# A two-layer decoder trunk: gate and up products with the activations stationary, the FFN's pre-gain in the weights, bias products over 128 rows, and eight weight splits on GpSimd

## The chip, the cores and the metric

The kernel runs on one core of a Trainium2 chip. The metric is device microseconds of one execution. Lower is better. TensorE runs at one of two clock levels, 1.2 or 2.4 GHz; the profile gives the granted clock as a share of 2.4 GHz.

## The reference

The input is 256 rows of 1024 numbers. Two layers follow one another; each is FFN, mixer, FFN, and every sub-layer has an RMS norm before and after it. Cut to what matters here:

```python
def rms_norm(x, g):
    y = x * rsqrt(mean(x * x, axis=-1) + 1e-6)
    return y * g

def swiglu_ffn(h, w_gate_up, w_down):            # 1024 -> 2 x 2816 -> 1024
    gate, up = split(h @ w_gate_up, 2)
    return (silu(gate) * up) @ w_down

for layer in range(2):
    x = x + 0.5 * rms_norm(swiglu_ffn(rms_norm(x, fpre[layer, 0]), ...), fpost[layer, 0])
    h = rms_norm(x, mpre[layer])
    y = conformer_conv(h) if layer == 0 else attention(h, shared_kv(x))
    x = x + rms_norm(y, mpost[layer])
    x = x + 0.5 * rms_norm(swiglu_ffn(rms_norm(x, fpre[layer, 1]), ...), fpost[layer, 1])
```

The convolution layer is `(h @ w_in + b_in)` with a gate, a depthwise convolution of 31 taps, a layer norm, and `silu(u) @ w_out + b_out`. All is float32.

## The kernel before

**Products.** A float32 product is made of three products of a faster format (fp32r): each operand is split into a high part and a low part, and `mm3` (lines 185 to 189) adds high x high, high x low and low x high into one PSUM tile. The high part is a copy by ScalarE, the low part a subtraction by VectorE.

**Weights.** All weights lie in one tensor `wpk` of 320 pieces of 128 x 1024 numbers (512 KB), in the order in which `plan` (line 56) lists them. SyncE's queue loads a piece into one of 4 `raw` buffers (line 154); `split_piece` makes `whi` (ScalarE, line 172) and `wlo` (VectorE, line 174), two halves of 512 columns each, into one of 9 pairs of buffers. For the keys `k`, `q`, `v` of the attention the split also multiplies by a norm's gain (lines 167 and 168). `use` (line 177) loads and splits up to 10 pieces ahead of the one asked for. A `raw` buffer is free again when its split is done, a split buffer when TensorE has read it for the last time.

**The FFN** (`ffn`, line 296) has 22 blocks of 128 hidden columns. The normed rows stand transposed in `xT` (high and low, 1024 x 256). `gate_up` (line 324) makes one block for both halves of the rows at once: `unit` (line 275) keeps a 128 x 128 block of weights in the array and moves 256 columns of `xT` past it, 48 matmuls for a block. The result `pgu` stands already transposed, as the down product wants it: a silu, a product, a split, and it is `act`. The first block of the first FFN and the first three of the others are made by `gate_up_rows` (line 302) instead, one half of the rows (`tt`) at a time: there the rows are stationary, 256 columns of weights move, and two transposes a block (`pta`, line 318) turn the result. That lets the FFN begin when the first half of the rows is ready; `turn` (line 238) transposes the rows (`ptr`, line 244) into `xT`.

**The down product** (`down`, line 339) has the activations stationary and moves 512 columns of weights; it follows its block by two blocks or more. Of the second half of the rows the last 7 blocks (`DEFER`) are put off to the end, where they cover the norms of the first half.

**Norms.** `chain` (line 379) makes the sub-layer's end for a half of the rows: `post_norm` (line 207) adds the normed result into `xs`, and `pre_norm` (line 223) scales `xs` by the reciprocal root (made by GpSimd, line 198) and, before an FFN, by the gain: `xg`, line 233, which `turn` transposes. A gain row is loaded by a DMA that repeats it over 128 partitions.

**The convolution layer** (`conv`, line 430) adds its biases by a matmul over 33 partitions (`bhl`, lines 450 and 523): the high part of the bias in one row, the low part 32 rows below, against ones. Its 16 input pieces (`cin`) are followed by 8 output pieces (`cout`). `filter_` makes the convolution by a Fourier product (`pU`, `prod`, `ys`, `y`), `layer_norm` normalizes `y` into `z`, and its reciprocal root `re` is made by GpSimd (line 503).

The instructions of an engine run in the order of its queue. A scheduler sets that order from the program's order and from priorities (`high_priority`, `issue_after`).

Of the kernel before, what the change touches and what calls it, by code (L numbers as in the profile page):

```python
# [47 lines left out]
GAINS_AT = 10  # L48
POOL_SPLITS = ()
VTURN = 1  # L50
FTURN = 7
FLEAD = (1, 3, 3, 3)
# [3 lines left out]
def plan():  # L56

    order = []
    for f in (0, 1, 2, 3):
        for i in range(NF):  # L60
            order += [("gu", f, i, 0), ("gu", f, i, 1)]
            if i % 2 == 1 and i >= 3:
                order += [("dn", f, i - 3), ("dn", f, i - 2)]
# [5 lines left out]
        if f == 2:  # L69
# [9 lines left out]
GAINS = ["fpre0", "fpost0", "mpre0", "mpost0", "fpre1", "fpost1",  # L79
         "fpre2", "fpost2", "mpost1", "fpre3", "fpost3"]  # L80
# [17 lines left out]
def trunk(ctx, tc, x, wpk, gains, pvec, dft, wdw, bvec, out):  # L98
# [5 lines left out]
    t2 = ctx.enter_context(tc.tile_pool(name="t2", bufs=12))  # L104
    gpool = ctx.enter_context(tc.tile_pool(name="gpool", bufs=3))
# [29 lines left out]

    load_x(0)
    pv = const.tile([P, NPV], F32, name="pv")
    load_gain("fpre0")
# [9 lines left out]
    def load_piece():  # L148

        i = state["next"]  # L150
        state["next"] += 1
        key = order[i]
        raw = wraw.tile([P, HW], F32, name="raw", tag="raw")
        nc.sync.dma_start(raw, wpk[i])
        return lambda: split_piece(key, raw, nc.gpsimd if i in POOL_SPLITS else nc.vector)

    def split_piece(key, raw, eng):
# [3 lines left out]
        if key[0] in ("k", "q", "v"):  # L161
            gname = "gq" if key[0] == "q" else "gkv"
            parts = [(key[1], 0, HW)] if key[0] == "v" else [
                (4 * key[2] + j, 256 * j, 256) for j in range(4)]
            for k, o, n in parts:
                g = pcol(gname, k)
# [34 lines left out]
    def sumsq(src):  # L201
        junk = t2.tile([P, 512], F32, name="junk", tag="junk", bufs=1)
# [18 lines left out]
    normed = {}  # L221

    def pre_norm(tt, pre):
# [51 lines left out]
    def unit(p, w):  # L275

        for s in range(2):
            for k in range(KD):
                wh, wl = w[k // 4]
                c = ((k % 4) * 2 + s) * P  # L280
                mm3(p[:, s, :], wh[:, c:c + P], wl[:, c:c + P], xT[0][:, k, :], xT[1][:, k, :],
                    k == 0, k == KD - 1)

    def rows_unit(p, w, tt, final):


        for k in range(KD):
            if final and tt == 0 and k == FTURN:
                turn(1)
# [526 lines left out]
```

## Time and profile before

| | |
|---|---|
| runs | 996.59, 998.08, 999.80 us; median 998.08 |
| the profiled execution | 997.41 us |
| its span from the first to the last instruction | 995.6 us |
| TensorE matmul busy | 976.5 us (98% of the span) |
| VectorE busy | 605.5 us (61%) |
| ScalarE busy | 517.4 us (52%) |
| GpSimd busy | 19.1 us (2%) |
| HBM | 175.14 MB read, 177 GB/s over the span |
| granted TensorE clock | 0.996 in the mean, 0.5 in a stretch near the start |

The busy time of TensorE counts a matmul from its issue to its modelled end, and matmuls overlap. What a matmul costs is the distance from its start to the start of the next.

### The profile page before, as it was taken

The numbers are of one execution on the slowest core, as the hardware profiler recorded it, in microseconds if no ns is written. First come the engines' busy times: TensorE is split into PE (matmuls) and PEld (weight loads), VectorE is DVE, ScalarE is ACT, GpSimd is POOL, SyncE is SP. The second block draws the span as 40 slices with busy tenths as digits, with TensorE's granted clock in tenths as the row PEclk, the third lists the DMA queues.
The fourth block names the chain that finished last, engine by engine and source line by source line (L and its number), as shares of the span: only waits on it lengthen the run. The fifth ranks groups of instructions, "written<-read, shape, count | busy, mean of one in ns | idle before, by whom it ended". The sixth has DMA issues, their size and how long they took to land.

```text
span 995.6 us, 16742 instructions
## 1 busy us (share of the span) xinstructions
PE 976.5 (98%) x6470; PEld 884.3 (89%) x6470; DVE 605.5 (61%) x1136; ACT 517.4 (52%) x1083; POOL 19.1 (2%) x40
## 2 busy tenths in 40 slices
PE   7999999999989999999999999999999999999997
PEld 6998999976658999999899999998899899999996
DVE  5865454487568654545585454547887785454542
ACT  5755454473246554544564454546785565454541
POOL 0000000010001000000000000000000000000000
PEclk8999999999999999999999999999999999999999
DMA  6867565565226766665476566655654456666531
GB/s 234 293 216 245 156 173 187 162 198 169 92 78 211 214 190 189 181 198 165 141 240 206 184 190 191 173 162 185 202 160 122 142 172 210 190 180 199 172 106 43
DMA packets 49232, 177.27 MB, mean 178 GB/s; under 512 B 5593, under 2 KB 5593, under 8 KB 49152
## 3 DMA queue, kind: packets, MB, share of 16 engines
q1 hardware_dynamic: 49152, 176.21, 57.0%
q8 instruction: 50, 0.82, 0.3%
q14 instruction: 30, 0.25, 0.1%
HBM read 175.14 MB, written 1.05 MB: 177 GB/s over the span
## 4 chain that ended last, share of the span: by engine, by line
PE 89%; DVE 4%; DMA 2%; issue 2%; ACT 1%; POOL 1%; DVEq 0%; SPq 0%; POOLq 0%; ACTq 0%
PE pgu L187 15%; PE pgu L189 15%; PE pgu L188 15%; PE acc L271 9%; PE acc L272 9%; PE acc L273 9%; PE pgr L189 1%; PE pgr L187 1%; PE pgr L188 1%; PE pkq L189 1%; PE pkq L188 1%; PE pkq L187 1%; PE pag L187 1%; DVE wlo L174 1%; DMA raw<-in_wpk_dram 1%
## 5 line engine op out<-in xcount | busy, mean ns | idle before, releaser
L174 DVE TENSOR_TENSOR wlo<-raw,whi 128x512 fp32r<-128x512 f32 x592 | 389.3, 687 | 297.7 <-ACT whi L172 286.7
L172 ACT CAST whi<-raw 128x512 fp32r<-128x512 f32 x592 | 344.5, 618 | 334.1 <-PE pgu L188 124.6
L188 PE MATMUL pgu<-xTl,whi 128*128 128x256 f32 x1248 | 353.3, 283 | 0.2 <-DVE xTl L255 0.2
L189 PE MATMUL pgu<-xTh,wlo 128*128 128x256 f32 x1248 | 353.4, 283 | 0.0
L187 PE MATMUL pgu<-xTh,whi 128*128 128x256 f32 x1248 | 353.2, 283 | 0.0
L187 PEld LDWEIGHTS pgu<-xTh,whi 128*128 128x128 f32 x1248 | 239.5, 192 | 2.2 <-issue 0.8
L188 PEld LDWEIGHTS pgu<-xTl,whi 128*128 128x128 f32 x1248 | 239.4, 192 | 1.8 <-DVE xTl L255 0.4
L189 PEld LDWEIGHTS pgu<-xTh,wlo 128*128 128x128 f32 x1248 | 239.4, 192 | 0.0
L271 PE MATMUL acc<-whi,act 128*128 128x512 f32 x384 | 150.4, 392 | 0.0
L272 PE MATMUL acc<-whi,act 128*128 128x512 f32 x384 | 150.1, 391 | 0.0
L273 PE MATMUL acc<-wlo,act 128*128 128x512 f32 x384 | 149.6, 390 | 0.0
L273 PEld LDWEIGHTS acc<-wlo,act 128*128 128x128 f32 x384 | 72.1, 188 | 15.2
L271 PEld LDWEIGHTS acc<-whi,act 128*128 128x128 f32 x384 | 72.3, 188 | 13.7
L272 PEld LDWEIGHTS acc<-whi,act 128*128 128x128 f32 x384 | 72.3, 188 | 13.1
L188 PE MATMUL pgr<-wlo,xTh 128*128 128x256 f32 x160 | 46.7, 293 | 0.2 <-DVE wlo L174 0.2
L187 PE MATMUL pgr<-whi,xTh 128*128 128x256 f32 x160 | 46.5, 292 | 0.2 <-ACT whi L172 0.2
L189 PE MATMUL pgr<-whi,xTl 128*128 128x256 f32 x160 | 45.8, 291 | 0.1
L333 ACT CAST act<-af 128x256 fp32r<-128x256 f32 x78 | 31.7, 407 | 23.9 <-DVE af L331 23.8
L167 ACT ACTIVATE whi<-raw,pv 128x256 fp32r<-128x256 f32 (+1 forms) x72 | 36.5, 573 | 7.5 <-PE pgu L188 2.5
L168 DVE SCALAR_TENSOR_TENSOR wlo<-raw,pv,whi 128x256 fp32r<-128x256 f32 (+1 forms) x72 | 37.2, 568 | 5.0 <-ACT whi L167 5.0
L188 PE MATMUL pkq<-xTl,whi 128*128 128x256 f32 x128 | 36.5, 285 | 0.0
L187 PE MATMUL pkq<-xTh,whi 128*128 128x256 f32 x128 | 36.5, 285 | 0.0
(125 smaller groups left out, 949.0 us busy)
## 6 DMA issues: line engine op xcount, KB each, us to landing
raw<-in_wpk_dram SPq DMA_DIRECT2D x320, 512.0 KB, 4.3
gain<-in_gains_dram SPq DMA_DIRECT2D x11, 512.0 KB, 5.8
xs<-in_x_dram SPq DMA_DIRECT2D x4, 256.0 KB, 2.7
out_dram<-xs SPq DMA_DIRECT2D x4, 256.0 KB, 2.0
dm<-in_dft_dram SPq DMA_DIRECT2D x1, 368.0 KB
taps<-in_wdw_dram SPq DMA_DIRECT2D x1, 124.0 KB
braw<-in_bvec_dram SPq DMA_DIRECT2D x6, 4.0 KB
ys<-in_bvec_dram SPq DMA_DIRECT2D x2, 2.0 KB
```

The costliest lines, as they stand in the source:

```text
L167: nc.scalar.activation(hi[:, o:o + n], raw[:, o:o + n], AF.Copy, scale=g)
L168: nc.vector.scalar_tensor_tensor(lo[:, o:o + n], raw[:, o:o + n], g, hb[:, o:o + n], op0=ALU.mult, op1=ALU.subtract)
L172: nc.scalar.copy(hi[:, o:o + 512], raw[:, o:o + 512])
L174: eng.tensor_sub(lo[:, o:o + 512], raw[:, o:o + 512], hb[:, o:o + 512])
L187: nc.tensor.matmul(out_ap, wh, xh, start=start, stop=False)
L188: nc.tensor.matmul(out_ap, wh, xl, start=False, stop=False)
L189: nc.tensor.matmul(out_ap, wl, xh, start=False, stop=stop)
L271: nc.tensor.matmul(o, xh, wh[:, cols], start=first, stop=False)
L272: nc.tensor.matmul(o, xl, wh[:, cols], start=False, stop=False)
L273: nc.tensor.matmul(o, xh, wl[:, cols], start=False, stop=last)
L333: nc.scalar.copy(hl[:, 0, :], a)
```

## The change

**FFN.** All blocks are now made by `gate_up` in pairs (256 gate and 256 up columns), one half of the rows at a time, with the rows stationary and 512 columns of weights moving. A pair takes 4 pieces, each with two k-blocks of 512 columns, and both halves of the rows read them. `turn_act` transposes the pair's product (4 transposes of 128 x 128, now for every pair), and one copy and one subtraction of 512 columns make `ahi` and `alo`. The FFN's pre-norm no longer makes `xg`: `turn` transposes `xs` as it is; the gain is multiplied into the gate and up weights in the split (a column `gc` of a small table), and the reciprocal root `rstds` into the silu and the product after it. The first pair (first FFN) or two pairs (the others) are made for the first half of the rows, then `turn(1)`, then for the second half. At the FFN's end one deferred down block (`COVERED`) is moved ahead of the last pair's down blocks, since these now wait for `turn_act`.

**Bias product.** The ones and the bias rows stand in 128 partitions, filled with zeros, and the matmul takes all 128.

**Splits on GpSimd.** The low parts of the 8 `cout` pieces (16 subtractions of 128 x 512) are made by GpSimd. The memsets for the bias rows go to GpSimd too.

**Buffers and loads.** `t2` has 14 buffers for 12, the gains 2 for 3, `junk` 2 for 1. Four gain rows of 512 KB are no longer loaded.

```diff
-GAINS_AT = 10
-POOL_SPLITS = ()
+GAINS_AT = 5
+POOL_SPLITS = ("cout",)
-FTURN = 7
-FLEAD = (1, 3, 3, 3)
+FLEAD = (1, 2, 2, 2)
+COVERED = 1
...
-        for i in range(NF):
-            order += [("gu", f, i, 0), ("gu", f, i, 1)]
-            if i % 2 == 1 and i >= 3:
-                order += [("dn", f, i - 3), ("dn", f, i - 2)]
+        for i in range(NF // 2):
+            order += [("gu", f, i, q) for q in range(KD // 2)]
+            if i >= 1:
+                order += [("dn", f, 2 * i - 2), ("dn", f, 2 * i - 1)]
...
+    gc = const.tile([P, NGC], F32, name="gc")
+    nc.sync.dma_start(gc, gcol)
     load_x(0)
     pv = const.tile([P, NPV], F32, name="pv")
-    load_gain("fpre0")
...
-        return lambda: split_piece(key, raw, nc.gpsimd if i in POOL_SPLITS else nc.vector)
+        return lambda: split_piece(key, raw, nc.gpsimd if key[0] in POOL_SPLITS else nc.vector)
...
+        if key[0] in ("gu", "k", "q", "v"):
+            if key[0] == "gu":
+                parts = [(gc[:, key[1] * KD + k:key[1] * KD + k + 1], 512 * (k % 2), 512)
+                         for k in (2 * key[3], 2 * key[3] + 1)]
...
+            for g, o, n in parts:
                 nc.scalar.activation(hi[:, o:o + n], raw[:, o:o + n], AF.Copy, scale=g)
                 nc.vector.scalar_tensor_tensor(lo[:, o:o + n], raw[:, o:o + n], g, hb[:, o:o + n],
                                                op0=ALU.mult, op1=ALU.subtract)
...
+        if pre == "ffn":
+            normed[tt] = xs[:, tt, :].rearrange("p (h n) -> p h n", h=2)
         s = [sumsq(xs[:, tt, h * 512:(h + 1) * 512]) for h in range(2)]
-        r, _ = rstd_of(s[0], s[1], 1.0 / D, RMS_EPS)
+        r, last = rstd_of(s[0], s[1], 1.0 / D, RMS_EPS)
+        if pre == "ffn":
+            rstds[tt] = r
+            return last
...
+        def gate_up(i, tt):
+
+            if i not in raws:
+                raws[i] = ([use(("gu", f, i, q)) for q in range(KD // 2)],
+                           t2.tile([P, NT, 2 * P], F32, name="ar", tag="t2"))
+            w, a = raws[i]
+            p = ps.tile([P, 2, 2 * P], F32, name="pgu", tag="mm")
+            rows_unit(p.rearrange("p a b -> p (a b)"), w, tt)
             with tc.high_priority(offset=400):
+                s = t2.tile([P, 2 * P], F32, name="sg", tag="sg", bufs=2)
+                nc.scalar.activation(s, p[:, 0, :], AF.Silu, scale=rstds[tt])
+                nc.vector.scalar_tensor_tensor(a[:, tt, :], p[:, 1, :], rstds[tt], s, op0=ALU.mult, op1=ALU.mult)
+
+        def turn_act(i):
+
+            a = raws.pop(i)[1]
+            pt = ps.tile([P, 2, T], F32, name="pta", tag="tr")
+            for tt in range(NT):
+                for j in range(2):
+                    nc.tensor.transpose(pt[:, j, tt * P:(tt + 1) * P], a[:, tt, j * P:(j + 1) * P], ident)
             with tc.high_priority(offset=400):
+                hi, lo = (t2.tile([P, 2, T], F32R, name=n, tag="t2") for n in ("ahi", "alo"))
+                nc.scalar.copy(hi, pt)
+                nc.vector.tensor_sub(lo, pt, hi.bitcast(F32))
...
+        for i in range(FLEAD[f]):
+            gate_up(i, 0)
+        turn(1)
+        for i in range(FLEAD[f]):
+            gate_up(i, 1)
+            if i:
+                turn_act(i - 1)
+        for i in range(FLEAD[f], NP):
...
+            gate_up(i, 0)
+            turn_act(i - 1)
+            gate_up(i, 1)
+            if i == FLEAD[f]:
+                for j in range(i - 1):
+                    down_pair(j, range(NT))
+            down_pair(i - 1, range(NT))
+        turn_act(NP - 1)
+        late = list(range(NF - DEFER, NF - TAIL))
+        for j in late[:COVERED]:
+            down(j, 1)
+        down_pair(NP - 1, (0,))
         after(0, acc[0])
-        for j in range(NF - DEFER, NF - TAIL):
+        for j in late[COVERED:]:
...
-            nc.tensor.matmul(flat, onesr[at, :], bhl[0][at, (q % 2) * 512:(q % 2 + 1) * 512],
+            nc.tensor.matmul(flat, onesr[:, q // 2, :], bhl[0][:, (q % 2) * 512:(q % 2 + 1) * 512],
...
-                nc.tensor.matmul(acc[tt][h], onesr[:33, :], bhl[1][:, h * 512:(h + 1) * 512],
+                nc.tensor.matmul(acc[tt][h], onesr[:, 0, :], bhl[1][:, h * 512:(h + 1) * 512],
...
-    with tc.issue_after(pre_norm(0, "fpre0").ins):
-        last = turn(0, between=first[:1])
+    pre_norm(0, "ffn")
+    last = turn(0, between=first[:1])
```

**What moves on the engines.** Three places, as the two programs have them.

TensorE in the middle of the second FFN. Before, the gate and up matmuls of a block (`pgu`, 256 columns) go straight over into the down matmuls (`acc`):

```order
L187 MATMUL pgu<-xTh,whi 128x256
L188 MATMUL pgu<-xTl,whi 128x256
L189 MATMUL pgu<-xTh,wlo 128x256
L271 MATMUL acc<-whi,act 128x512
L272 MATMUL acc<-whi,act 128x512
```

Now the four transposes of the pair before (`pta`) stand between the first and the second half of the rows:

```order
L193 MATMUL pgu<-whi,xTl 128x512
L319 MATMUL pta<-ident,ar 128x128 x4
L191 MATMUL pgu<-whi,xTh 128x512
L192 MATMUL pgu<-wlo,xTh 128x512
L193 MATMUL pgu<-whi,xTl 128x512
```

The matmuls have 512 columns for 256 and are half as many, and a pair has 4 transposes that no block there had before.

GpSimd's queue from the first FFN to the attention, as a difference (`rr` and `re` are the reciprocal roots of the norms, `braw` and `ones` the constants of the bias product, `wlo` the low parts):

```order
-L198 TENSOR_TENSOR rr<-rb,nhalf 128x1 x2
-L409 MEMSET ones 97x128
-L198 TENSOR_TENSOR rr<-rb,nhalf 128x1 x4
-L503 TENSOR_TENSOR re<-ve,nhalf 128x1 x2
-L558 IOTA dist 128x256 x2
```

This stood there before. Now the same stretch has the following, which the difference shows as added:

```order
+L422 MEMSET braw 128x1024 x2
+L412 MEMSET ones 128x256
+L416 MEMSET ones 1x128 x4
+L202 TENSOR_TENSOR rr<-rb,nhalf 128x1 x4
+L178 TENSOR_TENSOR wlo<-raw,whi 128x512 x12
+L509 TENSOR_TENSOR re<-ve,nhalf 128x1
+L178 TENSOR_TENSOR wlo<-raw,whi 128x512 x4
+L509 TENSOR_TENSOR re<-ve,nhalf 128x1
```

The first `re` of the layer norm now stands behind twelve of the sixteen subtractions, the second behind all.

VectorE at the layer norm of the convolution layer, where TensorE waits for it (`z` is the normed `y`, `u` the gated input, `prod` and `ys` the convolution's products). Before:

```order
L506 TENSOR_SCALAR z<-y,mv,re 128x512 x2
L174 TENSOR_TENSOR wlo<-raw,whi 128x512 x2
L460 TENSOR_TENSOR u<-pag,sg 128x256
L174 TENSOR_TENSOR wlo<-raw,whi 128x512 x2
L481 TENSOR_TENSOR prod<-pU,spec_1143 80x512
```

Now:

```order
L507 TENSOR_SCALAR ve<-mv 128x1
L512 TENSOR_SCALAR z<-y,mv,re 128x512 x2
L466 TENSOR_TENSOR u<-pag,sg 128x256
L172 SCALAR_TENSOR_TENSOR wlo<-raw,gc,whi 128x512 x2
L487 TENSOR_TENSOR prod<-pU,spec_892 80x512
```

The subtractions ahead of `u` are gone; two of the next FFN's first piece stand ahead of `prod`.

## Rows read from the trace of the kernel before

**Rows 1.** The page: busy time of each engine with its share of the span and its instructions; and the chain that ended last, as shares of the span.

```profile
PE 976.5 (98%) x6470; PEld 884.3 (89%) x6470; DVE 605.5 (61%) x1136; ACT 517.4 (52%) x1083; POOL 19.1 (2%) x40
...
PE 89%; DVE 4%; DMA 2%; issue 2%; ACT 1%; POOL 1%; DVEq 0%; SPq 0%; POOLq 0%; ACTq 0%
```

**Rows 2.** The timeline of TensorE in the second FFN, from one down stretch over 96 gate and up matmuls to the next: start in us, duration in us, engine, line, operation, out<-in, columns.

```profile
403.32 0.40 PE L271 MATMUL acc<-whi,act 128*128 128x512 f32 x1
...
404.71 0.39 PE L271 MATMUL acc<-whi,act 128*128 128x512 f32 x1
...
408.79 0.28 PE L187 MATMUL pgu<-xTh,whi 128*128 128x256 f32 x1
...
420.30 0.40 PE L271 MATMUL acc<-whi,act 128*128 128x512 f32 x1
```

**Rows 3.** Groups of instructions: line, engine, operation, names, shape, count | busy us, mean ns of one | idle us before them. The groups L187 and L189 have the same counts as L188.

```profile
L188 PE MATMUL pgu<-xTl,whi 128*128 128x256 f32 x1248 | 353.3, 283 | 0.2 <-DVE xTl L255 0.2
...
L188 PE MATMUL pgr<-wlo,xTh 128*128 128x256 f32 x160 | 46.7, 293 | 0.2 <-DVE wlo L174 0.2
...
L318 PE MATMUL pta<-ident,ar 128*128 128x128 f32 x20 | 6.1, 303 | 1.8 <-DVE ar L314 1.8
```

**Rows 4.** The timeline of TensorE at the end of the convolution layer, where eight transposes stand in a stream of 512-column matmuls.

```profile
305.69 0.39 PE L273 MATMUL acc<-wlo,xTh 128*128 128x512 f32 x1
305.92 1.03 PE L244 MATMUL ptr<-ident,xg 128*128 128x128 f32 x8
...
307.03 0.40 PE L272 MATMUL acc<-whi,xTl 128*128 128x512 f32 x1
```

**Rows 5.** The timeline of TensorE around one bias matmul of the convolution layer, and the group of all eight.

```profile
230.94 0.39 PE L189 MATMUL pag<-whi,xTl 128*128 128x512 f32 x1
231.26 0.50 PE L450 MATMUL pag<-bhl,onesr 33*128 33x512 f32 x1
231.69 0.50 PE L187 MATMUL pag<-whi,xTh 128*128 128x512 f32 x1
232.02 0.39 PE L188 MATMUL pag<-wlo,xTh 128*128 128x512 f32 x1
```
```profile
L450 PE MATMUL pag<-bhl,onesr 33*128 33x512 f32 x8 | 4.0, 495 | 0.0
```

**Rows 6.** The start: the timeline of all engines (a bracket gives the idle time before and what ended it), and a row of TensorE's timeline from the second block on.

```profile
1.65 0.42 SPq L125 DMA_DIRECT2D gain<-in_gains_dram  x1
...
8.87 1.41 DVE L233 SCALAR_TENSOR_TENSOR xg<-xs,rr,gain 128x512 f32<-128x512 f32 x2 [2.63 <-DMA gain<-in_gains_dram]
9.67 1.66 PE L244 MATMUL ptr<-ident,xg 128*128 128x128 f32 x8 [2.30 <-DVE xg L233]
...
12.37 0.63 ACT L204 ACTIVATE junk<-xs 128x512 f32<-128x512 f32 x1
```
```profile
29.82 0.28 PE L187 MATMUL pgu<-xTh,whi 128*128 128x256 f32 x1
```

**Rows 7.** The start in stretches of 2 us: stretch and length, busy us (count) of TensorE, its weight loads, VectorE, ScalarE and GpSimd, then the granted clock, the share of the DMA engines and GB/s.

```profile
6.00:8.00 2.00, 1.37 (x4) 0.68 (x2) 0.16 (x1) 0.04 (x1) 0.55 (x1) 1.00 0.93 354
...
12.00:14.00 2.00, 1.78 (x9) 1.67 (x9) 1.90 (x5) 2.00 (x5) 0.00 (x0) 0.50 0.84 319
```

**Rows 8.** The chain that ended last at the end of the first FFN: start in us, us, what.

```profile
198.62 0.24 PE acc L273
...
205.69 0.76 DVE xg L233
206.50 0.65 PE ptr L244 x4
```

**Rows 9.** All waits of TensorE for `xg` (us in total, times, longest), and one of them in its timeline, at the start of the second FFN.

```profile
PE ptr L244 <- DVE xg L233: 5.3, 6, 2.3
```
```profile
318.65 1.29 PE L244 MATMUL ptr<-ident,xg 128*128 128x128 f32 x8 [0.69 <-DVE xg L233]
```

**Rows 10.** The layer norm of the convolution layer: the timeline of VectorE, and of ScalarE (the high parts of the second and of the sixth `cout` piece).

```profile
274.21 1.53 DVE L506 TENSOR_SCALAR z<-y,mv,re 128x512 f32<-128x512 f32 x2 [0.66 <-POOL re L503]
275.66 1.28 DVE L174 TENSOR_TENSOR wlo<-raw,whi 128x512 fp32r<-128x512 f32 x2
276.86 0.42 DVE L460 TENSOR_TENSOR u<-pag,sg 128x256 f32<-128x256 f32 x1
...
278.45 2.48 DVE L481 TENSOR_TENSOR prod<-pU,spec 80x512 f32<-80x512 f32 x4
```
```profile
254.31 1.14 ACT L172 CAST whi<-raw 128x512 fp32r<-128x512 f32 x2 [1.63 <-PE pag L189]
...
268.22 1.14 ACT L172 CAST whi<-raw 128x512 fp32r<-128x512 f32 x2 [3.35 <-PE pag L189]
```

**Rows 11.** Durations: groups of VectorE, ScalarE and GpSimd with shapes kept apart, and the DMA of a piece (count, KB each, median us to landing).

```profile
L174 DVE TENSOR_TENSOR wlo<-raw,whi 128x512 fp32r<-128x512 f32 x592 | 389.3, 687 | 297.7 <-ACT whi L172 286.7
...
L168 DVE SCALAR_TENSOR_TENSOR wlo<-raw,pv,whi 128x1024 fp32r<-128x1024 f32 x8 | 10.2, 1280 | 3.1 <-ACT whi L167 3.1
...
L219 DVE SCALAR_TENSOR_TENSOR xs<-pn,rr,xs 128x512 f32<-128x512 f32 x24 | 17.1, 754 | 1.8 <-POOL rr L198 0.6
...
L560 POOL TENSOR_SCALAR_AFFINE_SELECT dist<-dist 128x256 f32<-128x256 f32 x2 | 0.8, 400 | 0.0
```
```profile
raw<-in_wpk_dram SPq DMA_DIRECT2D x320, 512.0 KB, 4.3
```

More of the change, by code (lines that the diff above doesn't have):

```diff
@@ L76, in plan @@
     return order
[L79 to L80 removed]
+GAINS = ["fpost0", "mpre0", "mpost0", "fpost1", "fpost2", "mpost1", "fpost3"]
+NGC = 4 * KD
 PV = {}
@@ L97, in trunk @@
 @with_exitstack
-def trunk(ctx, tc, x, wpk, gains, pvec, dft, wdw, bvec, out):
+def trunk(ctx, tc, x, wpk, gains, gcol, pvec, dft, wdw, bvec, out):
     nc = tc.nc
@@ L273, in rows_product, with rows_unit @@
             nc.tensor.matmul(o, xh, wl[:, cols], start=False, stop=last)
[L275 to L284, printed above, removed]
+    def rows_unit(p, w, tt):
         for k in range(KD):
-            if final and tt == 0 and k == FTURN:
-                turn(1)
-            wh, wl = w[k // 4]
-            c = slice((k % 4) * 2 * P, (k % 4 + 1) * 2 * P)
+            wh, wl = w[k // 2]
+            c = slice((k % 2) * 512, (k % 2 + 1) * 512)
             xh, xl = (xT[j][:, k, tt * P:(tt + 1) * P] for j in range(2))
@@ L324, in gate_up @@
-        def gate_up(i):
-            p = ps.tile([P, 2, T], F32, name="pgu", tag="mm")
-            unit(p, [use(("gu", f, i, hh)) for hh in range(2)])
-            with tc.high_priority(offset=400):
-                s = t2.tile([P, T], F32, name="sg", tag="sg", bufs=2)
-                nc.scalar.activation(s, p[:, 0, :], AF.Silu)
-                a = t2.tile([P, T], F32, name="af", tag="af", bufs=2)
-                nc.vector.tensor_mul(a, s, p[:, 1, :])
-                hl = t2.tile([P, 2, T], F32R, name="act", tag="t2")
-                nc.scalar.copy(hl[:, 0, :], a)
-                nc.vector.tensor_sub(hl[:, 1, :], a, hl[:, 0, :].bitcast(F32))
-            act[i] = hl
+        raws = {}
@@ L342, in down, with down_pair @@
             wh, wl = wd[i]
-            hl = act[i]
-            rows_product(acc, tt, hl[:, 0, tt * P:(tt + 1) * P], hl[:, 1, tt * P:(tt + 1) * P],
-                         wh, wl, i == 0, i == NF - 1, halves)
-        done = 0
+            hi, lo = act[i]
+            cols = slice(tt * P, (tt + 1) * P)
+            rows_product(acc, tt, hi[:, cols], lo[:, cols], wh, wl, i == 0, i == NF - 1, halves)
+        def down_pair(i, tts):
+            for j in (2 * i, 2 * i + 1):
+                for tt in tts:
+                    if tt == 0 or j < NF - DEFER:
+                        down(j, tt)
+        NP = NF // 2
         if 0 in normed:
             turn(0)
-        for tt in range(NT):
-            for i in range(FLEAD[f]):
-                gate_up_rows(i, tt)
-        for i in range(NF):
+        for i in range(FLEAD[f]):
[6 more added lines that the diff above has]
+        for i in range(FLEAD[f], NP):
             if i == GAINS_AT:
```

89 lines of the change are left out of this document (32 added, 57 removed).

## The prediction

> **What bounds the kernel now.** I read the page first. TensorE is busy for 98% of the span, and the chain that ended last runs on it for 89%; VectorE and ScalarE are busy for 61% and 52%, GpSimd for 2% [rows 1]. So TensorE's stream is priced, and every other engine only at the places where TensorE waits. Since busy times overlap (a matmul of 256 columns is given 283 ns, one of 512 columns some 390), I next read the distance from start to start in the middle of an FFN. From 408.79 to 420.30 lie 96 matmuls of 256 columns: 11.51 / 96 = 0.1199 us each. The 18 matmuls of 512 columns from 404.71 to 408.79 take 4.08 us, 0.2267 each, and the 24 from 403.32 take 5.47, 0.2279 each [rows 2]. A column thus costs 0.468 ns at 256 and 0.443 to 0.445 at 512. The third look was at the few stretches in which TensorE doesn't stream: the start, the ends of the FFNs and the layer norm of the convolution layer. The change touches all of them.
>
> **Gate and up.** Removed are 3 x 1248 matmuls `pgu` and 3 x 160 `pgr` [rows 3], 4224 of 256 columns: 4224 x 0.1199 = 506.5 us. Added are 2112 of 512 columns at 0.2275 (between the two values above): 480.5 us. That is **-26.0** (-25.2 to -27.7 by the two values).
>
> **Transposes.** An FFN has 11 pairs with 4 transposes each, 176 in all, against 20 `pta` now [rows 3]: 156 more. Their own row is no price, since the first ones waited. Eight transposes do stand in a running stream of 512-column matmuls: from 305.69 to 307.03 are 1.34 us with two matmuls and eight transposes [rows 4], so 1.34 - 2 x 0.2267 = 0.887, or 0.111 each. 156 x 0.111 = **+17.3**. Four in a row may cost more by one than eight do, as their beginning and end weigh more: a bound is +0.3 per group, which is about half of the 0.65 us that a group of four took alone at an FFN's end [rows 8]. That bound is a rival below. Copies and subtractions of 512 columns replace two of 256 each on ScalarE and VectorE; both have room, and in a pair's middle the down product that needs them comes 24 matmuls (5.4 us) later.
>
> **Bias product.** The matmul over 33 partitions and the one before and the one after it take 232.02 - 230.94 = 1.08 us from start to start; three matmuls of the stream take 0.68 [rows 5]. The row over 33 partitions thus costs 0.40 more than a plain one. If 128 partitions make it plain, eight of them give 3.2 and the four output biases, of which no row stands alone, some 0.3: **-3.5**. The bounds are 0 (the extra belongs to something else, for instance to its place at a product's start) and -4.8 (12 x 0.40). Padding and memsets lie on GpSimd before that layer, where it has nothing to do. The Trainium skill ("TensorE: Matmul & The Clock Gate", section "Why this matters for your kernels") says that a single matmul over 32 partitions takes the same time as one over 128. By this the padding would give nothing and the sum would be 3.5 us worse. The row disagrees.
>
> **The start.** TensorE's first transposes waited 2.30 us for `xg`, and this waited 2.63 for the gain's DMA, issued at 1.65 [rows 6]. Now `xs` is transposed as it lands; the 512 KB of the gain are not loaded, which at the 354 GB/s of that stretch [rows 7] brings every weight piece 512 / 354 = 1.5 us forward. The table of gains is small and goes first. On the other side the clock was at its upper level from 6 to 8 and at its lower level (0.50, 1.2 GHz) from 12 to 14 [rows 7], though TensorE worked in both: work that comes earlier falls into the same slow time in part. A pair also asks for four pieces and for a split with a scale, and ScalarE was full there (2.00 of 2.00 us [rows 7]). Two blocks, 96 matmuls, were done at 29.82 [rows 6]; I expect the first pair, the same work, at about 26.3. **-3.5**: the 2.30 of the wait and most of the 1.5. Bounds: 0 (ScalarE and the slow clock keep all) and -6 (the wait, the 1.41 of `xg` and the 1.5, and a shorter slow stretch).
>
> **Ends and beginnings of FFNs.** At an end the last pair's transposes now stand before its down product. One deferred down block, 6 x 0.2267 = 1.36 us, covers the copy (0.57, half of 1.14 [rows 10]) and the subtraction (0.69 [rows 11]); with three hand-overs at 0.05 to 0.1 (`xg` ended at 206.45, its reader began at 206.50 [rows 8]) and the transposes' own end the cover is short by some 0.3: four times, +1.2. The covering block is taken from those that hide the first half's norm. At the end of the first FFN this norm runs from 198.86 to 206.45 and the transposes follow it at once [rows 8], so it had no slack. The new order leaves two matmuls fewer between the end of the sum and these transposes: 2 x 0.2267 = 0.45, at the convolution and at the attention, the two places where `xg` stays: +0.9. At the three FFN beginnings the scaled rows are no longer on the path: the wait for `xg` there was 0.69 in the row [rows 9], 2.1 for three; I take half, as the other waits in that total are shorter: -1.0. Sum **+1.1**, bounds -3 (all waits for `xg` but the start's, 5.3 - 2.3 [rows 9]) and +6 (1 us more at each of six places).
>
> **Splits.** The subtractions of gate and up become operations with a scalar: 0.64 for 512 columns by the row of 1024 (1.28), 0.75 by another with the same operands, against 0.69 [rows 11]; 352 of them move VectorE by -17 to +24 us of work, which stays beside the stream: 0. The eight `cout` pieces take 16 x 0.69 = 11 us off VectorE and put 16 subtractions on GpSimd. No row shows one there. Nearest are GpSimd's 256 columns at 0.40, 0.80 for 512, and VectorE's 0.69 [rows 11]; I take 0.8. What they could delay is `re`, queued behind twelve of them, for which VectorE (`z`) and behind it TensorE wait. The second piece's high part was ready at 255.45, the sixth's at 269.36, and `re` was due at 273.55, where VectorE began to wait [rows 10]. Ten subtractions in 18.1 us: from 1.8 us each on `re` comes late, and 0.8 is far below. The Trainium skill ("GPSIMD Engine Reference", section 3.1, "Elementwise") gives 4497 ns for 2048 elements of such an operation; a quarter is 1.12 us, an estimate by that page, also below. VectorE, on its side, loses two or four subtractions (1.28 a pair) ahead of `u` and `prod` [rows 10], and gets two of the next FFN in their place. I count **0**, between -1 and +3.
>
> **The sum.** -26.0 + 17.3 - 3.5 - 3.5 + 1.1 = -14.6. The profiled execution took 997.41, 995.6 of it the span, so 982.8; the median of the runs is 0.67 higher: **983.5**.
>
> **The rivals.** (a) All uncertain terms end well: bias -4.8, start -6, ends 0, matmuls at 0.2267: 998.1 - 27.7 + 17.3 - 4.8 - 6 = **977**. For it: the wait for `xg` in the start is large. Against: the slow clock. (b) Start and ends give nothing or cost: start 0, ends +5: 983.5 + 3.5 + 3.9 = **991**. For it: four new hand-overs, each at a place where the cover was measured to be just enough. (c) GpSimd is late, or holds VectorE up: each of 16 subtractions blocks a VectorE operation, of which only those in the layer norm's chain reach TensorE: +3, **987**. The Trainium skill ("SBUF — State Buffer", section "SBUF: two separate sides") describes a port that VectorE and GpSimd share, held by one of them for a whole instruction. No row of before has both at work on such operands, so it is open. (d) The bias matmul stays dear: **987**. (e) No change: a group of four transposes costs 0.3 us more than half of what eight cost. 44 x 0.3 = 13, and -14.6 shrinks to -1.4: **997**. For it: the product stands in PSUM as a whole only after a hand-over, and `pta` must wait for VectorE's product of the half before; against: in the order it stands 24 matmuls behind that, and the eight at 305.92 show no such price. (f) Slower: the weights starve. Both halves of the rows read a pair's four pieces, so 4 of 9 split buffers are held through the first half (24 x 0.2275 = 5.5 us) and none comes free; then they come free one every 1.37 us. A `raw` buffer waits for its split, this for a buffer, and the next load, 4.3 us to landing [rows 11], for `raw`. I count some 3 us of slack between a landing and its use. If each of the some 41 pairs in the steady state waited, from 14.6 / 41 = 0.36 us a pair the gain would be gone, and at 1 us the time is 983.5 + 41 = **1025**. Against it: six pieces a pair are 3.1 MB in 16.8 us, 187 GB/s, where the start moved 354, and the pieces asked for are ten ahead.
>
> **How the numbers follow.** Chances: forecast 0.57; (a) 0.08; (b) 0.10; (c) 0.08; (d) 0.05; (e) 0.08; (f) 0.04. The range of 8 in 10 takes in the forecast with its bounds and (a) to (d): 975 to 993. What this kernel's measurement can tell from no change is 0.3%, 3 us: faster means below 995.1. Faster are the forecast and (a) to (d), 0.88; within 0.3% is (e), 0.08; slower is (f), 0.04.
>
> **What would show each step.** In the profile after: 512-column `pgu` 0.2267 to 0.2279 apart; a group of `pta` 0.44 longer than two matmuls without it (0.75 would be (e)); the bias matmul with its neighbours 0.68, not 1.08; the first pair done near 26.3; idle times of TensorE of about 0.3 behind `pta` at the four FFN ends and 0.6 before `ptr` at the convolution; `z` waiting no longer for `re` than 0.66. Idle times of `pgu` after `whi` or `wlo`, in every pair, would be (f); `pta` waiting for `ar` inside the FFN would make the transposes dearer than 0.111. The forecast is wrong if the distance of the matmuls depends on which operand is stationary more than on the columns.

## The result, and the profile after

The changed kernel takes 981.9 us (median of 4 runs, 980.67 to 983.77), the kernel before 998.51 beside it: a ratio of 0.9837, 95% interval 0.9814 to 0.9860. The profiled execution took 980.67 us with a span of 978.9.

The page of the changed kernel, busy times and chain, as in [rows 1]:

```profile
PE 960.8 (98%) x4514; PEld 787.8 (80%) x4514; DVE 612.5 (63%) x1048; ACT 550.8 (56%) x1029; POOL 43.0 (4%) x62
...
PE 92%; DVE 3%; ACT 2%; DMA 1%; issue 1%; POOL 0%; DVEq 0%; POOLq 0%; ACTq 0%
```

TensorE is still the bound, with 16 us less of it. Where the time went is read by stretches, cut at the starts of the first and last gate and up matmuls in TensorE's timeline (us of the profiled executions):

| stretch | before | after | difference |
|---|---|---|---|
| start to the end of the first pair (two blocks before) | 29.82 | 21.96 | -7.86 |
| rest of gate and up, first FFN | 163.96 | 162.54 | -1.42 |
| end of the first FFN and convolution layer | 115.75 | 118.42 | **+2.67** |
| gate and up, second FFN | 174.49 | 170.47 | -4.02 |
| end of the second FFN | 16.82 | 16.66 | -0.16 |
| gate and up, third FFN | 173.61 | 170.49 | -3.12 |
| end of the third FFN and attention | 125.47 | 125.48 | +0.01 |
| gate and up, fourth FFN | 174.08 | 170.48 | -3.60 |
| end of the fourth FFN | 21.61 | 22.37 | +0.76 |
| sum | 995.61 | 978.87 | -16.74 |

The middle of an FFN, TensorE's timeline, which answers to [rows 2, 4]:

```profile
399.63 0.39 PE L193 MATMUL pgu<-whi,xTl 128*128 128x512 f32 x1
...
404.39 0.39 PE L193 MATMUL pgu<-whi,xTl 128*128 128x512 f32 x1
404.62 0.60 PE L319 MATMUL pta<-ident,ar 128*128 128x128 f32 x4
404.97 0.48 PE L191 MATMUL pgu<-whi,xTh 128*128 128x512 f32 x1
405.29 0.39 PE L192 MATMUL pgu<-wlo,xTh 128*128 128x512 f32 x1
...
410.53 0.39 PE L282 MATMUL acc<-whi,ahi 128*128 128x512 f32 x1
```

From 399.63 to 404.62 are 22 matmuls, 4.99 / 22 = 0.2268 each; from 405.29 to 410.53 are 23, 0.2278 each. A group of four transposes with its two neighbours takes 405.29 - 404.39 = 0.90, so 0.90 - 2 x 0.2268 = 0.446, or 0.111 a transpose. Nothing waits there.

What TensorE waited for in the whole span, by the view of waits (us in total, times, longest):

```profile
PE pz L517 <- DVE prod L487: 3.2, 2, 2.7
PE ptr L255 <- DVE xg L244: 1.8, 2, 1.0
PE ptr L255 <- DVE xTl L266: 1.5, 1, 1.5
...
PE pU L481 <- DVE u L466: 0.9, 1, 0.9
PE ptr L255 <- DVE xg L242: 0.8, 1, 0.8
PE pgu L191 <- ACT xTh L265: 0.7, 3, 0.2
...
```

The wait for `xg` that stood at every FFN start [rows 9] is gone from these (0.24 us for `xTh` is left at each). The longest wait is a new one: 2.7 us for `prod`, in the layer norm of the convolution layer. The timeline of TensorE, VectorE and GpSimd there, which answers to [rows 10]:

```profile
259.86 1.12 PE L494 MATMUL y<-ys,dm 81*128 81x512 f32 x2 [0.16 <-DVE ys L488]
261.53 1.13 PE L494 MATMUL y<-ys,dm 80*128 80x512 f32 x2 [0.55 <-DVE ys L489]
267.01 1.94 PE L481 MATMUL pU<-u,dm 128*80 128x512 f32 x4 [0.93 <-DVE u L466]
271.64 0.66 PE L517 MATMUL pz<-ident,z 128*128 128x128 f32 x4 [2.69 <-DVE prod L487]
272.84 1.11 PE L517 MATMUL pz<-ident,z 128*128 128x128 f32 x4 [0.54 <-DVE prod L487]
```
```profile
258.36 1.44 DVE L488 TENSOR_TENSOR ys<-prod 80x512 f32<-80x512 f32 x1
259.73 1.75 DVE L489 TENSOR_TENSOR ys<-prod 80x512 f32<-80x512 f32 x1
...
264.49 1.53 DVE L512 TENSOR_SCALAR z<-y,mv,re 128x512 f32<-128x512 f32 x2 [0.66 <-POOL re L509]
...
267.14 3.25 DVE L172 SCALAR_TENSOR_TENSOR wlo<-raw,gc,whi 128x512 fp32r<-128x512 f32 x2 [0.19 <-ACT whi L171]
270.31 2.47 DVE L487 TENSOR_TENSOR prod<-pU,spec 80x512 f32<-80x512 f32 x4
```
```profile
257.99 1.27 POOL L178 TENSOR_TENSOR wlo<-raw,whi 128x512 fp32r<-128x512 f32 x1 [3.05 <-ACT whi L176]
257.99 2.94 POOL L178 TENSOR_TENSOR wlo<-raw,whi 128x512 fp32r<-128x512 f32 x2 [3.05 <-ACT whi L176]
...
264.42 5.42 POOL L178 TENSOR_TENSOR wlo<-raw,whi 128x512 fp32r<-128x512 f32 x4
```

`re` is not late: `z` waits for it 0.66 us, as before. But `ys` takes 1.44 and 1.75 us, and the two low parts of the next FFN's weights 3.25 together, just while GpSimd subtracts. (The second GpSimd row holds the first.) `prod` behind them begins at 270.31, and TensorE stands 2.69 us.

### The profile page after: what moved, and what is told of

The parts are those of the page before. It is cut to its first block, busy times and chain, and to the rows that moved or that the text cites. A ratio compares the mean times of both kernels' runs of the same rounds, so it can differ in the third digit from the quotient of the medians.

```text
span 978.9 us, 12711 instructions
## 1 busy us (share of the span) xinstructions
PE 960.8 (98%) x4514; PEld 787.8 (80%) x4514; DVE 612.5 (63%) x1048; ACT 550.8 (56%) x1029; POOL 43.0 (4%) x62
## 4 chain that ended last, share of the span: by engine, by line
PE 92%; DVE 3%; ACT 2%; DMA 1%; issue 1%; POOL 0%; DVEq 0%; POOLq 0%; ACTq 0%
PE pgu L191 16%; PE pgu L193 16%; PE pgu L192 16%; PE acc L283 10%; PE acc L282 10%; PE acc L284 10%; PE pta L319 2%; PE pkq L192 1%; PE pkq L193 1%; PE pkq L191 1%; PE pag L191 1%; PE pag L193 1%; PE pag L192 1%; DMA raw<-in_wpk_dram 1%; DVE wlo L172 1%
## 5 line engine op out<-in xcount | busy, mean ns | idle before, releaser
L172 DVE SCALAR_TENSOR_TENSOR wlo<-raw,gc,whi 128x512 fp32r<-128x512 f32 x352 | 249.1, 753 | 92.9 <-ACT whi L171 89.8
L171 ACT ACTIVATE whi<-raw,gc 128x512 fp32r<-128x512 f32 x352 | 234.1, 717 | 99.1 <-PE acc L283 62.2
L191 PE MATMUL pgu<-whi,xTh 128*128 128x512 f32 x704 | 278.2, 395 | 0.7 <-ACT xTh L265 0.7
L192 PE MATMUL pgu<-wlo,xTh 128*128 128x512 f32 x704 | 274.5, 390 | 0.1
L193 PE MATMUL pgu<-whi,xTl 128*128 128x512 f32 x704 | 274.0, 390 | 0.0
L176 ACT CAST whi<-raw 128x512 fp32r<-128x512 f32 x240 | 137.1, 619 | 46.4 <-PE pag L193 19.3
L178 DVE TENSOR_TENSOR wlo<-raw,whi 128x512 fp32r<-128x512 f32 x224 | 145.1, 686 | 18.3 <-ACT whi L176 17.6
L283 PE MATMUL acc<-whi,alo 128*128 128x512 f32 x352 | 137.5, 391 | 0.2 <-DVE alo L323 0.2
L282 PE MATMUL acc<-whi,ahi 128*128 128x512 f32 x352 | 137.4, 390 | 0.0
L284 PE MATMUL acc<-wlo,ahi 128*128 128x512 f32 x352 | 137.2, 390 | 0.0
L283 PEld LDWEIGHTS acc<-whi,alo 128*128 128x128 f32 x352 | 66.1, 188 | 14.8 <-DVE alo L323 1.4
```

Of the source, the lines that this page charges most:

```text
L171: nc.scalar.activation(hi[:, o:o + n], raw[:, o:o + n], AF.Copy, scale=g)
L172: nc.vector.scalar_tensor_tensor(lo[:, o:o + n], raw[:, o:o + n], g, hb[:, o:o + n], op0=ALU.mult, op1=ALU.subtract)
L176: nc.scalar.copy(hi[:, o:o + 512], raw[:, o:o + 512])
L178: eng.tensor_sub(lo[:, o:o + 512], raw[:, o:o + 512], hb[:, o:o + 512])
L191: nc.tensor.matmul(out_ap, wh, xh, start=start, stop=False)
L192: nc.tensor.matmul(out_ap, wh, xl, start=False, stop=False)
```

## The experiments

Twelve kernels, run in three groups; each ratio is to the kernel before, run beside the group. "us" from ratios: 0.001 is 1 us.

**Cout pieces back on VectorE** (`e1_no_pool`).

```diff
-POOL_SPLITS = ("cout",)
+POOL_SPLITS = ()
```

> The changed kernel, with the low parts of the eight cout pieces made by VectorE again. Theory 1 (GpSimd's subtractions hold up VectorE's operations with two SBUF inputs, there ys at 1.44 and 1.75 us for 0.68 and the weights' low parts at 1.58 and 1.75 for 0.75): these durations fall back to 0.68 and 0.75, TensorE's wait for prod before the first pz falls from 2.69 to about 0.5, its two waits for ys (0.16, 0.55) go, and without that long idle time the granted clock stays up after 272 us. Time 2.5 to 6 us below the changed kernel. Theory 2 (the durations belong to something else, and 16 subtractions back on VectorE make u and prod later): the waits stay or grow, time equal or up to 2 us above.

976.56 us, ratio 0.9794 (0.9777 to 0.9811), some 4.3 us below the changed kernel's 0.9837. VectorE and TensorE at the same place:

```profile
258.43 0.68 DVE L488 TENSOR_TENSOR ys<-prod 80x512 f32<-80x512 f32 x1
259.03 0.68 DVE L489 TENSOR_TENSOR ys<-prod 80x512 f32<-80x512 f32 x1
...
271.17 1.41 DVE L172 SCALAR_TENSOR_TENSOR wlo<-raw,gc,whi 128x512 fp32r<-128x512 f32 x2
```
```profile
266.45 1.94 PE L481 MATMUL pU<-u,dm 128*80 128x512 f32 x4 [1.55 <-DVE u L466]
268.91 0.66 PE L517 MATMUL pz<-ident,z 128*128 128x128 f32 x4 [0.52 <-DVE prod L487]
270.11 0.66 PE L517 MATMUL pz<-ident,z 128*128 128x128 f32 x4 [0.54 <-DVE prod L487]
```

The durations are back at 0.68 and 0.70, the wait for `prod` at 0.52. `u` is later, as theory 2 said (TensorE waits 1.55 for it against 0.93), by less than the hold costs. The granted clock belongs to it: the windows of 4 us over this place, first of the changed kernel, then of this one (the columns of [rows 7]):

```profile
268.00:272.00 4.00, 1.31 (x6) 0.45 (x5) 4.00 (x5) 1.02 (x1) 1.84 (x2) 1.00 0.63 226
272.00:276.00 4.00, 3.46 (x10) 1.98 (x9) 2.32 (x5) 3.01 (x8) 0.00 (x0) 0.57 0.49 162
276.00:280.00 4.00, 4.00 (x10) 2.41 (x9) 2.42 (x6) 0.00 (x0) 0.04 (x1) 0.57 0.00 0
```
```profile
268.00:272.00 4.00, 2.94 (x12) 1.51 (x12) 4.00 (x8) 2.40 (x7) 0.00 (x0) 1.00 0.63 207
272.00:276.00 4.00, 3.53 (x14) 2.21 (x13) 3.27 (x9) 0.50 (x2) 0.55 (x1) 1.00 0.44 131
```

With GpSimd TensorE is busy for 1.31 of 4 us, and then the clock is at its lower level, half of 2.4 GHz, for 6.8 us; without, it stays up. Of the 118.42 - 113.70 = 4.7 us by which the stretch (end of first FFN and convolution layer) is shorter here, 2.9 are lost by the second `pz`, where the clock falls: it begins 88.34 us after the last gate and up matmul of the first FFN (at 184.50) with GpSimd, and 85.48 (after 184.63) without. The longer waits for `ys` and `prod` make most of that. The other 1.9 lie behind it, where the clock is down; no run parts the clock from what else is slower there. The two come together: all six profiled executions of the changed FFN with the eight pieces on GpSimd have such a slow stretch behind this layer norm, and none of the five with no piece or five pieces there has one.

**Only the first five pieces on GpSimd** (`e8_pool5`): `key[0] in POOL_SPLITS and key[1] < 5`.

> The changed kernel with the low parts of only the first five of the eight cout pieces on GpSimd, those that it made before 255 us, when VectorE had no operation with two SBUF inputs under way; the last three are on VectorE. Theory 1 (the hold matters only where it meets ys and the weights' low parts, at 258 to 270): the waits of TensorE for ys go and that for prod falls to some 0.5, time as with no piece on GpSimd or up to 1 below. Theory 2 (what costs is any use of GpSimd there): like the changed kernel.

977.0 us, ratio 0.9789 (0.9776 to 0.9803): as without any. The waits for `ys` are gone, those for `prod` are 0.5. Ten subtractions on GpSimd between 235 and 256 us cost nothing, and they gain nothing either: VectorE has room there.

**Bias over 33 partitions** (`e2_bias33`).

```diff
-            nc.tensor.matmul(flat, onesr[:, q // 2, :], bhl[0][:, ...],
+            at = slice(64 * (q // 2), 64 * (q // 2) + 33)
+            nc.tensor.matmul(flat, onesr[at, q // 2, :], bhl[0][at, ...],
```

(and `[:33]` in the output bias.)

> The changed kernel with the bias matmuls over 33 partitions as before (same tiles, only the slice read). Theory 1 (33 partitions cost 0.40 us more with the neighbours, 8 times, and the four output biases a little): 3.5 us above the changed kernel, and 1.08 us from the matmul before the bias to the second after it, where 128 partitions have 0.68. Theory 2 (the place at a product's start costs it, not the partitions): no difference. A value between, about 2, if only the bias matmul's own distance to the next (0.42 for 0.23) belongs to the partitions.

Ratio 0.9866 (0.9843 to 0.9888): 2.9 us above the changed kernel, within what the intervals leave open. The rows settle it. TensorE's timeline here, and then of the changed kernel:

```profile
224.65 0.39 PE L193 MATMUL pag<-whi,xTl 128*128 128x512 f32 x1
224.97 0.50 PE L457 MATMUL pag<-bhl,onesr 33*128 33x512 f32 x1
...
225.73 0.39 PE L192 MATMUL pag<-wlo,xTh 128*128 128x512 f32 x1
```
```profile
221.90 0.39 PE L193 MATMUL pag<-whi,xTl 128*128 128x512 f32 x1
222.13 0.39 PE L456 MATMUL pag<-bhl,onesr 128*128 128x512 f32 x1
...
222.58 0.39 PE L192 MATMUL pag<-wlo,xTh 128*128 128x512 f32 x1
```

1.08 us against 0.68, at the same place of a product: 33 partitions cost 0.40 us more each.

**The FFN's change alone** (`e14_ffn_only`): both edits above together.

> The FFN's change alone: the changed kernel with bias matmuls over 33 partitions and no piece on GpSimd. If the parts add up (bias -3, GpSimd +4.5 against the changed kernel): some 979 to 980 where the kernel before takes 997, and 2.5 to 3.5 above the kernel with no piece on GpSimd. If the bias part gains only beside the GpSimd part: as the kernel with no piece on GpSimd.

980.19 us, ratio 0.9830 (0.9818 to 0.9843); against no piece on GpSimd with the padded bias 0.9794, so the padding gives 3.6 us here too. The three parts are FFN -17.0, bias -3.6 and GpSimd +4.3. They are steps along one row of kernels, so their sum proves nothing; that the padding is worth about the same with GpSimd's pieces (2.9) and without (3.6) does. Part of the 3.6 belongs to the clock: this profiled execution has a slow stretch in the first FFN, from 93.8 to 97.2. In the stretch with the convolution layer, where neither has one, it is 116.29 against 113.70, 2.6 us.

**Every transpose twice** (`e3_turns_twice`): `for j in (0, 1, 0, 1)` around the transpose.

> The changed kernel with every transpose of a pair issued twice (8 in a group, 176 more). Theory 1 (a transpose costs 0.111 us at the margin): 19 to 20 us above the changed kernel. Theory 2 (transposes cost more by a group than by one): the group of four takes over 0.44 beyond the two matmuls around it, and the 176 more still cost 19 us or less. If the added ones came out at 0.18 or more, 32 us above.

1001.98 us, ratio 1.0049 (1.0031 to 1.0067), 21 us above the changed kernel. In the trace the distance within a group is 0.109; 176 x 0.109 = 19.2. The rest goes with the clock in the profiled execution: gate and up of the three later FFNs are each 4.3 us longer than in the changed kernel, that of the first FFN 7.0 (169.51 for 162.54), with a slow stretch from 95.3 to 102.2 in it, and another stands in the start.

**256 moving columns** (`e4_cols256`).

```diff
+        for o in (0, 256):
...
-                mm3(p, xh, xl, wh[:, c], wl[:, c], k == 0, k == KD - 1)
+                mm3(p[:, o:o + 256], xh, xl, wh[:, c], wl[:, c], k == 0, k == KD - 1)
```

(`c` now spans the 256 columns at `o`, and the loop over `k` stands inside.)

> The changed kernel with 256 moving columns a matmul in gate and up (rows still stationary, twice as many matmuls and weight loads, same order of work otherwise). Theory 1 (a column costs more in a matmul of 256, whichever operand is stationary): 4224 matmuls at 0.120, +26 us, between +25 and +28. Theory 2 (the gain comes from which operand is stationary, or from fewer waits for weights): +5 or less. If weight loads of 128 columns cannot hide behind 256 moving columns of this order: well over +28.

1015.95 us, ratio 1.0183 (1.0167 to 1.0199): 34.5 us above the changed kernel. By the time alone the last of the expectations would fit, but the stream itself is at 0.120 a matmul, as theory 1 has it. In the profiled execution gate and up of the second, third and fourth FFN take 177.57 us each for 170.48, 7.1 more, which is 28.4 for four, just above theory 1's 25 to 28. The rest lies at two places. The first pair ends 4.1 later (26.08 for 21.96): 2.6 us of waits stand behind its first matmul, as the first 256 columns ask for all four pieces in half the time. And the rest of gate and up in the first FFN is 9.8 longer, where its share of the columns is 6.5; a slow stretch of the clock from 98.4 to 105.3 lies in it.

**The start.** Three kernels. More warming matmuls in the kernel before, `WARM = 9` (`e5_before_warm9`) and `WARM = 15` (`e12_before_warm15`):

> The kernel before with nine warming matmuls for seven at its start, so that TensorE stands still some 0.6 us instead of 2.3 before its first transposes; nothing else is moved. Theory 1 (the start's gain in the changed kernel, 7.9 us to the first pair, is in good part the granted clock: before it was 0.50 from 10.5 to 17.3 us, after that long idle time): the clock stays at 1.00, the first two blocks are done some 3.4 us earlier (half of 6.83), the time is 2 to 4 us below the kernel before. Theory 2 (the start is limited by the weight pieces and their splits): the two blocks end at most 1 us earlier, the time is the same.

> The kernel before with 15 warming matmuls for seven, which at the two clock levels seen end near 9.5 us, where the first transposes begin; with nine they ended at 6.9, since the clock rose sooner, and the idle time and the slow stretch stayed. Theory 1 (the idle time ahead of the transposes brings the slow stretch at 10.5 to 17.3): idle time below 0.5, no slow stretch in the start, the first two blocks done 1 to 3.4 us earlier than 29.8, time 1 to 3 us below. Theory 2 (the clock there falls for another reason, the thin stretch of transposes and short waits behind it): the slow stretch stays, time equal or up to 1 us above.

With nine the clock rose sooner, the warming ended sooner, and the idle time was 2.66 us and the slow stretch as before: ratio 0.9996 (0.9985 to 1.0007), and nothing was learnt of the clock. With fifteen the idle time and the slow stretch of the start are gone, and the kernel is not faster: ratio 1.0017 (1.0004 to 1.0029). The ratio alone settles little, since the profiled execution has a slow stretch elsewhere, from 100.8 to 107.6, which costs 3.0 us there (rest of gate and up, first FFN: 166.97 for 163.96). The rows of the start do. One window over the start, 10 to 18 us, of the kernel before, with fifteen, and of the changed kernel:

```profile
10.00:18.00 8.00, 7.58 (x38) 6.65 (x36) 6.23 (x12) 6.50 (x15) 0.70 (x2) 0.57 0.73 268
```
```profile
10.00:18.00 8.00, 5.57 (x41) 4.57 (x39) 6.23 (x12) 7.18 (x16) 0.71 (x2) 1.00 0.68 242
```
```profile
10.00:18.00 8.00, 7.92 (x36) 5.85 (x35) 6.93 (x14) 7.21 (x14) 3.40 (x8) 1.00 0.76 271
```

At the full clock the kernel before does 41 matmuls for 38 in these 8 us and waits for the rest; its 97th gate and up matmul begins at 29.75 us, where it was 29.82 [rows 6]. Both theories fall: the slow stretch went with the idle time, as theory 1 said, but it had cost nothing, since TensorE would have waited in that time. (ScalarE's order moved too: the first `whi` begins at 11.35 for 10.85, but the sums of squares behind it at 12.39 for 12.37.) The changed kernel does 36 in the same stretch, most of them of twice the columns. What TensorE waited for in the first 30 us, first with fifteen and then of the changed kernel:

```profile
PE pta L318 <- DVE ar L314: 2.1, 2, 1.2
PE pgr L187 <- ACT whi L172: 1.2, 1, 1.2
...
PE ptr L244 <- DVE xg L233: 0.6, 1, 0.6
PE pgr L188 <- DVE wlo L174: 0.5, 1, 0.5
PE pgu L188 <- DVE xTl L255: 0.2, 1, 0.2
```
```profile
PE ptr L255 <- DVE xTl L266: 1.5, 1, 1.5
```

The chain that ended last, of the first 31 us, shows what these waits go back to: five of its rows in the kernel with fifteen, and the same load in the kernel before.

```profile
15.78 0.74 DVE xg L233
16.52 0.61 DVE wlo L174
...
17.15 6.89 DMA raw<-in_wpk_dram
...
24.06 0.63 ACT whi L172
...
25.41 0.30 DVE ar L314
```
```profile
17.13 7.08 DMA raw<-in_wpk_dram
```

On VectorE a `wlo` stands behind the `xg` of the second half. Its end frees a `raw` buffer for the sixth weight piece, which lands some 7 us later. The split of this piece stands ahead of the silu and of `ar`, and for `ar` the transposes of the second half's product wait. From the first half's transposes to these no matmul is in the chain, at either clock.

The gain's load ahead of the rows again (`e6_first_gain`): `load_gain("fpost0")` before `load_x(0)`.

> The changed kernel with one gain row (512 KB) loaded ahead of the input rows, as the kernel before did, and not later; nothing waits for it at the start. It shows what the bytes alone cost. Theory 1 (bytes: 512 KB at some 354 GB/s): xs and every weight piece land 1.5 us later and the first pair ends 1.5 us later. Theory 2 (the splits limit the start): below 0.5. Theory 3 (TensorE then idles longer before the transposes and the clock falls as in the kernel before): 4 us or more.

The first pair ends at 22.71 for 21.96, between theories 1 and 2; ratio 0.9845 (0.9831 to 0.9858), not told from 0.9837. TensorE stood 2.66 us ahead of the second half's transposes, and the clock stayed up. In other profiled executions of the changed FFN such an idle time stood at 2.16, 2.49 and 2.63 us without a slow stretch behind it and at 2.10 and 2.12 with one of 3.4 us: its length alone doesn't decide.

**The cover at the FFN's end.** `COVERED = 0` (`e9_cover0`), and a block of the pair before as the cover, without GpSimd (`e11_cover_own_no_pool`):

```diff
+        down(NF - 4, 0)
         turn_act(NP - 1)
-        for j in late[:COVERED]:
-            down(j, 1)
+        down(NF - 3, 0)
```

> The changed kernel with no deferred down block between the last pair's transposes and its down product. Theory 1 (the forecast's: copy and subtraction take some 1.6 us behind the transposes, which one block of 1.36 covers nearly): TensorE waits 1.3 to 1.6 us there at each of four FFN ends, 5 to 6.5 us, and gains the two waits for xg (0.78 and 0.84) back: 4 to 5 us above the changed kernel. Theory 2 (the down product begins on the high part, and the cover is hardly needed): 1 us above or below.

> No cout piece on GpSimd, and at the FFN's end the cover of the last pair's transposes is one down block of the pair before (six matmuls that stood ahead of the transposes) instead of a deferred block. The deferred blocks then all stand behind the first half's norm again. Expected against the kernel with no piece on GpSimd: the waits for xg at the ends of the first and the third FFN (0.77 and 0.85) go to 0.2 or less each, nothing new waits at the transposes (they wait for ar behind six matmuls, 1.36 us, for a silu and a product of 0.47 and 0.48): -1.0. If six matmuls don't hide the silu and the product: 0.2 to 0.5 at each of four ends, which takes the gain.

`COVERED = 0` came out at 982.99, ratio 0.9860 (0.9848 to 0.9873), 2.3 above the changed kernel. It was no test of an uncovered end: the scheduler put matmuls of the deferred blocks between the transposes and the last product by itself, no wait stands there, and later waits (1.54 for 1.02 before `turn(1)` at the convolution, 0.64, 0.24 and 0.72 for 0.84 before the attention) carry part of the time. The own cover: 977.21, ratio 0.9790 (0.9776 to 0.9805), as without it (0.9794). The waits for `xg` fell to 0.33 and 0.40 (0.2 or less was expected), but the next one, before the second half's transposes at the convolution, grew from 1.02 to 1.51, and the span from the end of the first pair on is only 0.16 us shorter. Half a microsecond was handed on, the rest isn't seen.

**Taps over 128 partitions** (`e13_pad_taps`), on top of the last kernel: `taps` and `dm` with all partitions, zeros below.

> No cout piece on GpSimd, the cover from the pair's own blocks, and the eight matmuls of the taps (psp, over 31 partitions, in the first FFN) over 128 partitions filled with zeros. In three of the runs on record the granted clock fell to 0.50 for 3.4 to 6.8 us right behind these eight. Theory 1 (matmuls over few partitions bring that): no slow stretch there in any run, granted clock 0.998 to 0.999 in all, the median 0 to 1 us below that of the kernel with 31 partitions. Theory 2 (it is the slow pace of these matmuls, 0.43 us each, whose both operands are unsplit float32): the stretch still comes in some runs, no difference.

976.63 us, ratio 0.9801 (0.9787 to 0.9815), no difference. No slow stretch stood behind these matmuls in its profiled execution, but none stood there either in six of the ten profiled executions of the changed FFN with 31 partitions, and the granted clock of its runs, 0.997 to 0.998, lies within the 0.995 to 0.999 of the last kernel, which has 31. It stays open.

## Why the prediction was right, and where it was not

The time forecast, 983.5 us against 981.9, is near for two reasons: the large terms held, and two small ones, the start and GpSimd, failed by 4.4 and 4.3 us in opposite directions. The second is luck.

- **Gate and up, -26.0: held.** 0.2268 and 0.2278 a matmul where 0.2275 was taken. With 256 columns and the same stationary rows the distance is 0.120 again: it is the columns, not the operand that is stationary, which was named as what could make the forecast wrong.
- **Transposes, +17.3: held.** A group costs 0.446 us in the rows, 44 x 0.446 - 20 x 0.111 = 17.4. Rival (e), 0.3 more a group, is out.
- **Bias, -3.5: held**, 0.40 us per matmul over 33 partitions in the row and 2.9 and 3.6 us by the two kernels that undo it (2.6 in the convolution layer's stretch). Rival (d) is out. The Trainium skill ("TensorE: Matmul & The Clock Gate", "Why this matters for your kernels") says that a single matmul over 32 partitions takes the same time as one over 128; by that, undoing the padding would have changed nothing. For 33 partitions within a stream over 128 the traces disagree, by 0.40 us each.
- **The start, -3.5: mis-sized.** It gave 7.9. The step that failed is that the slow clock was counted as a floor and the price was read from one wait, 2.30 for `xg`. The kernel with fifteen warming matmuls shows that these blocks ended at the same time at either clock: what held them was a row of waits, 1.24 for `whi` ahead of the first matmul, and behind it 0.53 for `wlo`, 0.62 for `xg` of the second half, 0.23 for `xTl`, 0.92 and 1.20 for `ar` before the transposes, 3.5 us together. The 0.62 and the 1.20 lie on the chain shown there, which runs over ScalarE, VectorE, GpSimd and a weight piece's load. In the changed kernel none of these stands behind the first matmul, since `turn(1)` needs no norm (it begins at 9.43 instead of 16.34), and a pair's transposes come after the next pair's first half. Against the kernel with fifteen, whose blocks are done at 29.75, the first matmul is 2.33 us earlier (9.70 for 12.03) and the waits are 3.5 less, 5.8 of 7.8; another 0.6 is the columns (96 x 0.1199 - 48 x 0.2275), and 1.4 isn't parted further (fewer transposes stand there). [rows 6, 7] had shown only the first link, with the slow clock hiding the others as busy time.
- **Ends and beginnings, +1.1: two parts as forecast, one not.** The waits for `xg` at the convolution and the attention grew from 0.17 and 0.36 to 0.78 and 0.84, +1.1 where +0.9 was said. At the three beginnings 0.69, 0.29 and 0.70 for `xg` became 0.24 each for `xTh`, -1.0 as said. The cover of the transposes was short by 0.05 at each of the four ends and not by 0.3: the down product begins on the high part, the low part is asked for one matmul later. That makes +0.3.
- **GpSimd, 0 between -1 and +3: wrong.** It costs 4.3 us. A subtraction takes 1.27 us where nothing meets it (257.99), so 0.8 was too low, but under 1.8, and `re` came in time. The step that failed is the "I count 0": rival (c) had the mechanism and was given 0.08 and 3 us. Its other half, the clock behind a TensorE that stands 2.7 us, was in no term.
- **Splits with a scalar and the held buffers: held.** No matmul of an FFN's stream waits for a weight; rival (f) is out.

With these values the sum is -26.0 + 17.4 - 3.5 - 7.9 + 0.3 + 4.3 = -15.4, or -14.8 without the 0.6 of columns that it counts twice. The ratio gives -16.3 (-14.0 to -18.6); the rest of 1.5 us isn't assigned.

The rule of the Trainium skill in (c) ("SBUF — State Buffer", "SBUF: two separate sides") says that whichever of the two engines begins first keeps the shared port for its whole instruction. The rows fit that: GpSimd's first subtraction ends at 257.99 + 1.27 = 259.26; `ys`, begun at 258.36, ends at 259.80, 0.54 behind that; GpSimd's second, held up by this, ends at 257.99 + 2.94 = 260.93, and the second `ys` ends at 259.73 + 1.75 = 261.48, 0.55 behind. `prod`, `u` and `z`, which read one operand from PSUM and at most one tile from SBUF, took under GpSimd's work what they take without it (four `prod` 2.48 from 235.38 on, beside subtractions from 234.25 to 236.76, and two `z` 1.53, both as in [rows 10]). That a hold of this kind is the cause is shown by moving the work (all of it, and the last three pieces alone); that it is this port and no other is the word of the Trainium skill, with which every row fits.

The best versions measured are the changed kernel without GpSimd's splits, or with five of them: 0.979 of the kernel before.

## What to carry to other kernels

Work given to an idle engine isn't free: check what the others do in that moment with two operands in SBUF, and move only what falls into a stretch without such operations; here ten subtractions were free and six cost 4 us. When a stretch shows a slow clock, count the waits that would stand there at full clock before pricing it. In a saturated TensorE stream the price of a form is the distance from start to start in a row of the same form, and it carried over to 0.3%.

## What the hardware showed that was not expected

A matmul over 33 partitions between matmuls over 128 costs 0.40 us more than one over 128. A granted clock of 0.5 for 6.8 us cost nothing where the engine was short of work, and 3.0 us in gate and up. GpSimd's own subtraction stretched too where it met VectorE's: the second of the pair from 257.99 on ended 1.67 us after the first (2.94 - 1.27), where a pair that meets none has 1.24 (2.51 - 1.27, from 234.25 on).
